# PEER block on one core: Exp, one-hot tiles, first gather rows, last two V tiles and the closing norm reordered

## The chip, the cores and the metric

The kernel runs on one NeuronCore of one Trainium2 chip. The metric is the device time of one execution in microseconds; lower is better. Only one core works, so there is no exchange between cores.

## The reference, cut to what matters

The layer is a token mixer (windowed attention beside a pooling branch, gated and merged) and then a PEER layer on 512 tokens of width 1024, with a final RMSNorm. In PEER every token picks, per head, 16 of 128 x 128 experts, and each expert is one row of `u_experts` and one row of `v_experts`:

```python
sv, si = lax.top_k(sc, PEER_TOPK)                      # per half of the key
fv, fi = lax.top_k(cand, PEER_TOPK)                    # of 256 sums
idx = jnp.take_along_axis(cidx, fi, axis=-1)
g = jax.nn.softmax(fv, axis=-1)
a = jax.nn.gelu(jnp.einsum('chkd,cd->chk', u_tab[idx], xc), approximate=False)
return jnp.einsum('chk,chkd->cd', g * a, v_tab[idx])
```

Everything is float32. The kernel has each float32 product as three matmuls of a high and a low part.

## The kernel before, in words

**The four token blocks.** The 512 tokens are four blocks of 128. Block 0 (`GB`) is computed by *gathering*: for each of its 128 (head, k) slots one indirect DMA on GpSimd brings 128 rows of `u_experts` (tile `row`, four buffers), VectorE forms the dot products (L715), and later 128 rows of `v_experts` are brought and added (L719). Blocks 1 to 3 are computed *densely*, against all 16384 experts: for each of 128 tiles of experts, `u_part` multiplies a U tile with the three blocks (24 matmuls, L105 to L107 with output `mm`) and ScalarE takes the Gelu (L604); `mix` multiplies by a gate tile (L640) and splits the product into high (L642, ScalarE) and low (L110, VectorE); `v_mm` multiplies it with the V tile into the accumulators `acc` (18 matmuls). Each U or V tile is loaded on SyncE's queue (L117), its high part is cast on ScalarE (L118), its low part taken on VectorE (L110). A token's gates are zero except at its 128 chosen experts.

**The stages.** Mixing and projections end near 360 us; `scores` near 475. In the *route* stage (to about 970 us) `part()` computes U tiles ahead of need, 4.3 us of TensorE each, and keeps their Gelu in SBUF or in HBM (`ahead`). Between the parts the program spends a budget of work on VectorE and ScalarE, by a cost that each step states: first `select` for block 0 (top-16, indices, softmax weights), then `select` and `onehot` for blocks 1 to 3 (the Background `bg`), and beside those the gathering (`fetch`, 1.1 units for each part, a dot or an add counts 1). `onehot` makes, in 16 builds per block, one-hot tiles `ohj` and `ohi` of eight tokens each; a matmul of the two (L584, output `pg`) is the gate tile, copied by ScalarE (L585) and stored to HBM. Every second `ohj` is made by ScalarE (eight Abs, L568, and a Relu, L569), the others by VectorE (L571). `ohi` is VectorE's (L574).

**The dense stage** begins with `open_dense` (the V tile and gate tiles of tile 0), six more parts (`TAIL`), the function `mix` that ends tile 0, and then `dense`, the loop over the V tiles. After it `final` makes the RMSNorm of each block: for each half an add of the accumulator (L742) and a Square with a sum (L743), the sum (L744), Sqrt (L745, another table of ScalarE than Gelu's or Exp's), a reciprocal (L746), and for each half the scaling (L748) and a store (L749).

**What sets the order.** Each engine runs its instructions in one fixed order. A planner makes it before the run: it keeps a reckoning of its own of when inputs are ready, gives each engine the instruction that is ready in that reckoning, and among several the one written earlier. `tc.high_priority(HP)` lets the U tiles of a part count as written earlier. `tc.issue_after(x)` puts what is written in its block behind the instruction x in the queue, for those instructions alone that run on the engine of x. `tc.manual_schedule` keeps the listed engines in the written order.

In `select`, `g` is the difference to the largest score (L517, VectorE); Exp (L525, ScalarE) is written ahead of the third of six pieces of the index search (L528 to L531, VectorE), and the sum of the weights (L535) behind the last.

Of the kernel before, what the change touches and what calls it, by code (L numbers as in the profile page):

```python
# [19 lines left out]
P = 128  # L20
# [29 lines left out]
G_B = 3.0  # L50
AHEAD = 60
HP = 400
U_S = 4
# [8 lines left out]
class Layer:  # L62
# [427 lines left out]
    def select(self, tp, sv, si, ei, g):  # L490
# [30 lines left out]
        for k0, k1, nh, pos, cand in ((0, 8, 4, self.fewpos, few), (8, 16, 2, self.iota[:, :NCAND], ce)):  # L521
            nk, w = k1 - k0, cand.shape[2]
            for h in range(0, PH, nh):
                if k0 == 8 and h == 0:
                    nc.scalar.activation(g, g, AF.Exp)  # L525
                hs, shape = slice(h, h + nh), [P, nh, nk, w]
                eq = tp.tile(shape, F32, name="eq", tag="k4", bufs=4)
                v.tensor_tensor(eq, pos.unsqueeze(1).unsqueeze(1).to_broadcast(shape),  # L528
                                ff[:, hs, k0:k1].unsqueeze(3).to_broadcast(shape), op=ALU.is_equal)
                v.tensor_tensor(eq, eq, cand[:, hs, :].unsqueeze(2).to_broadcast(shape), op=ALU.mult)  # L530
                v.reduce_sum(ef[:, hs, k0:k1], eq, axis=AX.X)  # L531
                yield (2.2 if k0 == 0 else 2.8) * SC
# [17 lines left out]
    def onehot(self, tp, c, jf, g):  # L550
# [12 lines left out]
        def build(n):  # L563
            u = 8 * n
            ohj = tp.tile([P, 8, P], F32, name="ohj", tag="k4", bufs=4)
            if n % OHN < OHA:
                for z in range(8):
# [30 lines left out]
    def u_part(self, n, w, xn2, keep=False):  # L598
# [3 lines left out]
        else:  # L602
            ga = self.ga.tile([P, TD], F32, name="ga", tag="ga", bufs=4)
        self.nc.scalar.activation(ga, ps, AF.Gelu)  # L604
        if keep and n >= RES:
# [10 lines left out]
    def gate_tile(self, n, q, parts=4):  # L616
        b = n // NI
        if q == 0:
# [3 lines left out]
                               in_=self.spill[s, :, n:n + NI, :].rearrange("g p i t -> p g (i t)"))  # L622

    def v_mm(self, n, w, v, acc):
        for c in range(ND):
            sl = slice(c * P, (c + 1) * P)
            for i in range(2):
                cl = slice(i * 512, (i + 1) * 512)
                self.mm3(acc[c][:, i, :], (w[0][:, sl], w[1][:, sl]), (v[0][:, cl], v[1][:, cl]),
                         n == 0, n == NKEY - 1)  # L630

# [34 lines left out]
    def dense(self, ahead, xn2, acc, fetch):  # L666
# [6 lines left out]
        def rate(m):  # L673
            return G_V if m < ahead else G_B

        last = NKEY - 2
        scale = (2 * PH * TOPK - fetch.spent) / sum(rate(m) for m in range(1, last))
        for m in (0, 1):
            u_load(m)
        for n in range(NKEY):  # L680
            m = n + 1
            if m == NKEY:
                pass
            elif m < ahead:
                step = self.mix(m, ahead)
# [7 lines left out]
            else:  # L693
# [4 lines left out]
                for _ in self.mix(m, ahead):  # L698
                    pass
            self.v_mm(n, self.ws.pop(n), self.vs.pop(n), acc)  # L700

    def gather(self, b, xn2, ei, g):
# [10 lines left out]
        def dot(s):  # L713
            u = rows(a["u_experts"], s)
            nc.vector.scalar_tensor_tensor(u, u, 1.0, xn2, op0=ALU.mult, op1=ALU.mult, accum_out=act[:, s:s + 1])  # L715

        def add(s):
            v = rows(a["v_experts"], s)
            nc.vector.scalar_tensor_tensor(z, v, act[:, s:s + 1], z, op0=ALU.mult, op1=ALU.add)  # L719

        for h in range(PH + 1):
            for k in range(TOPK):
# [11 lines left out]
    def final(self, b, y, g, acc=None):  # L734
        nc = self.nc
        t = self.rows.tile([P, D], F32, name="fin", tag="row")
        ss = self.s.tile([P, 2], F32, name="ssf")
        sd, r = (self.s.tile([P, 1], F32, name=n) for n in ("sdf", "rf"))
        halves = [slice(i * 512, (i + 1) * 512) for i in range(2)]
        for i, c in enumerate(halves):  # L740
            if acc is not None:
                nc.vector.tensor_tensor(y[:, c], acc[:, i, :], y[:, c], op=ALU.add)  # L742
            nc.scalar.activation(t[:, c], y[:, c], AF.Square, accum_out=ss[:, i:i + 1])  # L743
        nc.vector.tensor_tensor(ss[:, :1], ss[:, :1], ss[:, 1:], op=ALU.add)  # L744
        nc.scalar.activation(sd, ss[:, :1], AF.Sqrt, bias=self.eps, scale=1.0 / D)  # L745
        nc.vector.reciprocal(r, sd)  # L746
        for c in halves:
            nc.vector.scalar_tensor_tensor(t[:, c], y[:, c], r, g[:, c], op0=ALU.mult, op1=ALU.mult)  # L748
            nc.sync.dma_start(out=self.a["out"][0, b * P:(b + 1) * P, c], in_=t[:, c])  # L749

    def run(self):
# [60 lines left out]
        with tc.tile_pool(name="dense", bufs=2, reuse_waits="tile") as self.dp:  # L812
# [4 lines left out]
            nc.sync.dma_start(out=gf, in_=a["ln_final_g"].partition_broadcast(P))  # L817
            for _ in range(TAIL):
                with tc.issue_after(part()):
                    fetch.spend(G_A)  # L820
            mix()
            with tc.manual_schedule(engines={mybir.EngineType.PE, mybir.EngineType.DVE, mybir.EngineType.Activation}):
                self.dense(ahead, xn2, acc, fetch)
            fetch.spend(1e9)
            self.final(GB, self.hg, gf)
            for c in range(ND):
                hb = dp.tile([P, D], F32, name="hb", tag="vr", bufs=RAW)
                nc.sync.dma_start(out=hb, in_=self.hspill[c])
                self.final(DB + c, hb, gf, acc[c])

# [65 lines left out]
```

## Time and profile before

| | before |
|---|---|
| three runs | 1636.01, 1636.36 and 1644.2 us, median 1636.36 |
| profiled execution: span from the first to the last instruction | 1638.0 us |
| profiled execution: own time | not given beside the span; of the three runs only the one of 1644.2 us is longer than the span |
| TensorE (PE) busy | 1593.2 us |
| VectorE (DVE) busy | 1260.9 us |
| ScalarE (ACT) busy | 760.3 us |
| GpSimd (POOL) busy | 323.0 us |
| mean granted clock of TensorE | 0.992 |

All times are microseconds from the start of the span unless marked ns. A line of the timeline is start, duration, engine, line, operation, output and inputs, and in brackets the time for which the engine had stood idle before and what released it. An engine that waits in one instruction holds everything behind it in its queue. TensorE is busy for 97% of the span, so a change is worth what it takes from TensorE's idle time, or what it adds.

### The profile page before, as it was taken

To read this page: it belongs to the slowest core of one execution; us is meant where nothing else is said; L and a number is where in the kernel's file an instruction comes from. 1 tells how busy PE (TensorE), PEld (TensorE's weight loads), DVE (VectorE), ACT (ScalarE), POOL (GpSimd) and SP (SyncE) were. 2 spreads that over 40 slices of the span, in tenths; PEclk is the share of its full clock that TensorE was granted. 3 is DMA by queue.
4 is the path that set the end of the run, shared out by engine and by line. 5 is a ranking of instruction groups with operands and counts; after the bars stand their busy time and mean duration, and the time that the engine had idled before them with its cause. 6 is when DMAs were issued, how large, how long until landed. Compare 5 with 4: busy or idle time off the path is not lost.

```text
span 1638.0 us, 23397 instructions
## 1 busy us (share of the span) xinstructions
PE 1593.2 (97%) x8389; PEld 1411.9 (86%) x8389; DVE 1260.9 (77%) x2614; ACT 760.3 (46%) x1197; POOL 323.0 (20%) x262
## 2 busy tenths in 40 slices
PE   7999999999999899999999999999999999999997
PEld 6777788888899899999999998878888888899996
DVE  4676433546799899999999866877878878888885
ACT  4655533333333333894598863333333333433334
POOL 0000000000000334223322221221222222244440
PEclk9999999999999999999999999999999999999999
DMA  6111222531324888888988889999999999999983
GB/s 218 65 65 52 78 92 101 180 116 65 116 91 140 296 305 295 300 310 307 312 313 308 289 299 345 300 340 352 349 337 346 359 336 342 338 327 335 323 293 115
DMA packets 168117, 403.43 MB, mean 246 GB/s; under 512 B 14784, under 2 KB 87232, under 8 KB 164800
## 3 DMA queue, kind: packets, MB, share of 16 engines
q1 hardware_dynamic: 130384, 265.07, 46.1%
q0 software_dynamic: 36864, 134.23, 23.9%
q10 hardware_dynamic: 752, 2.62, 0.5%
q8 instruction: 66, 1.08, 0.3%
q14 instruction: 51, 0.42, 0.1%
HBM read 354.81 MB, written 46.53 MB: 245 GB/s over the span
## 4 chain that ended last, share of the span: by engine, by line
PE 86%; DMA 4%; DVE 4%; ACT 4%; issue 2%; SPq 0%; POOL 0%; DVEq 0%; ACTq 0%; POOLq 0%
PE mm L105 16%; PE mm L106 15%; PE mm L107 15%; PE acc L106 10%; PE acc L107 10%; PE acc L105 9%; PE pg L584 5%; DMA vr<-v_experts 2%; PE ho L105 1%; PE ho L107 1%; PE ho L106 1%; PE pss L453 1%; PE mm L368 1%; DVE wl L110 1%; ACT ohj L568 1%
## 5 line engine op out<-in xcount | busy, mean ns | idle before, releaser
L105 PE MATMUL mm<-xh,wh 128*128 128x384 f32 (+2 forms) x1424 | 503.3, 354 | 11.5 <-ACT ga L604 9.3
L107 PE MATMUL mm<-xh,wl 128*128 128x384 f32 (+2 forms) x1424 | 495.1, 348 | 1.9 <-DVE wl L110 1.9
L106 PE MATMUL mm<-xl,wh 128*128 128x384 f32 (+2 forms) x1424 | 494.8, 348 | 0.6 <-DVE xl L110 0.6
L110 DVE TENSOR_TENSOR wl<-wr,wh 128x1024 fp32r<-128x1024 f32 x187 | 228.0, 1220 | 135.7 <-ACT wh L118 123.0
L118 ACT CAST wh<-wr 128x1024 fp32r<-128x1024 f32 x187 | 195.6, 1047 | 284.9 <-PE mm L106 249.4
L709 POOL DMA_INDIRECT row<-u_experts,ei x128 | 150.0, 1172 | 885.5 <-ACT wh L118 528.2
L106 PE MATMUL acc<-vl,wh 128*128 128x512 f32 x768 | 299.9, 391 | 2.4 <-DVE vl L110 2.2
L107 PE MATMUL acc<-vh,wl 128*128 128x512 f32 x768 | 299.4, 390 | 0.0
L105 PE MATMUL acc<-vh,wh 128*128 128x512 f32 x768 | 298.8, 389 | 0.0
L105 PEld LDWEIGHTS mm<-xh,wh 128*128 128x128 f32 x1424 | 270.1, 190 | 31.0 <-ACT ga L604 10.7
L107 PEld LDWEIGHTS mm<-xh,wl 128*128 128x128 f32 x1424 | 269.8, 189 | 16.4 <-DVE wl L110 2.7
L106 PEld LDWEIGHTS mm<-xl,wh 128*128 128x128 f32 x1424 | 270.4, 190 | 13.8 <-DVE xl L110 1.1
L709 POOL DMA_INDIRECT row<-v_experts,ei x128 | 172.3, 1346 | 388.3 <-DVE hg L719 354.8
L642 ACT CAST wh<-wf 128x384 fp32r<-128x384 f32 x128 | 65.8, 514 | 322.5 <-PE acc L106 236.1
L110 DVE TENSOR_TENSOR vl<-vr,vh 128x1024 fp32r<-128x1024 f32 x128 | 156.7, 1224 | 52.8 <-ACT vh L118 49.7
L106 PEld LDWEIGHTS acc<-vl,wh 128*128 128x128 f32 x768 | 144.2, 188 | 33.9 <-DVE vl L110 4.6
L107 PEld LDWEIGHTS acc<-vh,wl 128*128 128x128 f32 x768 | 144.2, 188 | 29.8
L105 PEld LDWEIGHTS acc<-vh,wh 128*128 128x128 f32 x768 | 144.2, 188 | 29.5
L719 DVE SCALAR_TENSOR_TENSOR hg<-row,act,hg 128x1024 f32<-128x1024 f32 x128 | 163.6, 1278 | 2.9 <-DMA row<-v_experts,ei 2.5
L715 DVE SCALAR_TENSOR_TENSOR row<-row,natg 128x1024 f32<-128x1024 f32 x128 | 155.5, 1216 | 8.8 <-DMA row<-u_experts,ei 8.8
L118 ACT CAST vh<-vr 128x1024 fp32r<-128x1024 f32 x128 | 134.1, 1048 | 24.4 <-DMA vr<-v_experts 17.8
L110 DVE TENSOR_TENSOR wl<-wf,wh 128x384 fp32r<-128x384 f32 x128 | 74.0, 578 | 42.1 <-ACT wh L642 40.8
(179 smaller groups left out, 1611.6 us busy)
## 6 DMA issues: line engine op xcount, KB each, us to landing
wr<-u_blocks SPq DMA_DIRECT2D x128, 512.0 KB
vr<-v_experts SPq DMA_DIRECT2D x128, 512.0 KB
spill<-gs SPq DMA_DIRECT2D x24, 1024.0 KB
gt<-spill SPq DMA_DIRECT2D x64, 384.0 KB
ahead<-ga SPq DMA_DIRECT2D x90, 192.0 KB
gar<-ahead SPq DMA_DIRECT2D x90, 192.0 KB
wr<-w_in SPq DMA_DIRECT2D x30, 512.0 KB
wr<-w_query SPq DMA_DIRECT2D x16, 512.0 KB
```

The lines of the kernel that those rows point to most:

```text
L105: mm(out, lhsT=l[0], rhs=r[0], start=first, stop=False)
L106: mm(out, lhsT=l[0], rhs=r[1], start=False, stop=False)
L107: mm(out, lhsT=l[1], rhs=r[0], start=False, stop=last)
L110: self.lowered = self.nc.vector.tensor_tensor(lo, src, hi.bitcast(F32), op=ALU.subtract).ins
L118: self.nc.scalar.copy(hi, raw)
L368: nc.tensor.matmul(po[half * 64:half * 64 + 64], lhsT=vn[:, b - 1 + k, kv * 64:kv * 64 + 64], rhs=pT[:, k, 2 * half:2 * half + 2, :], star ...
L453: nc.tensor.matmul(pss[n][b // 2][:, b % 2, i - n, :], lhsT=qT[:, b * P:(b + 1) * P], rhs=subk[:, i, :], start=True, stop=True)
L584: nc.tensor.matmul(pg[:, z, :], lhsT=ohj[:, z, :], rhs=ohi[:, z, :], start=True, stop=True)
L642: nc.scalar.copy(wh, wf)
L709: nc.gpsimd.indirect_dma_start(out=t, out_offset=None, in_=tab, in_offset=bass.IndirectOffsetOnAxis(ap=ei[:, s:s + 1], axis=0))
L715: nc.vector.scalar_tensor_tensor(u, u, 1.0, xn2, op0=ALU.mult, op1=ALU.mult, accum_out=act[:, s:s + 1])
L719: nc.vector.scalar_tensor_tensor(z, v, act[:, s:s + 1], z, op0=ALU.mult, op1=ALU.add)
```

## The change

It has six edits. (1) In `select`, Exp is written two pieces later, inside `issue_after(seen)`, where `seen` is the `reduce_sum` (VectorE) of the piece before. (2) In `onehot` of the last block every fourth `ohj` is ScalarE's, not every second. (3) `gather` asks for its first four U rows ahead of everything and states a cost of 2.2 for it, so that the budget of two parts passes before the first dot; the total that `dense` spreads grows by the same 2.2. (4) The function `mix` is written inside `issue_after` of the Gelu of the fifth of the six `TAIL` parts. (5) The products of V tiles 126 and 127 are interleaved by accumulator: blocks 0 and 1 of the accumulators for both tiles, then the two halves of block 2; ahead of them stands a Sqrt of a constant. (6) `final` is cut into steps, and those of the three dense blocks are laid out in the order `CLOSE` on VectorE and ScalarE; the second half of each block is stored from ScalarE's queue.

```diff
+CLOSE = (0, 0, 0, 1, 1, 1, 2, 0, 2, 0, 1, 2, 0, 1, 2, 2, 1, 2, 0, 1, 2)
+FIRST = 2.2
...
-                if k0 == 8 and h == 0:
-                    nc.scalar.activation(g, g, AF.Exp)
+                if k0 == 8 and h == 4:
+                    with self.tc.issue_after(seen):
+                        nc.scalar.activation(g, g, AF.Exp)
...
-                v.reduce_sum(ef[:, hs, k0:k1], eq, axis=AX.X)
+                seen = v.reduce_sum(ef[:, hs, k0:k1], eq, axis=AX.X).ins
...
-            if n % OHN < OHA:
+            if n % (OHN if c + 1 < ND else 2 * OHN) < OHA:
...
-        self.nc.scalar.activation(ga, ps, AF.Gelu)
+        self.gelu = self.nc.scalar.activation(ga, ps, AF.Gelu).ins
...
-        scale = (2 * PH * TOPK - fetch.spent) / sum(rate(m) for m in range(1, last))
+        scale = (2 * PH * TOPK + FIRST - fetch.spent) / sum(rate(m) for m in range(1, last))
...
-            self.v_mm(n, self.ws.pop(n), self.vs.pop(n), acc)
+            if n < NKEY - 2:
+                self.v_mm(n, self.ws.pop(n), self.vs.pop(n), acc)
+        nc = self.nc
+        nc.scalar.activation(self.s.tile([P, 1], F32, name="sd"), self.eps, AF.Sqrt)
+        pair = [(n, self.ws[n], self.vs[n]) for n in (NKEY - 2, NKEY - 1)]
+        for part in ([(0, 0), (0, 1), (1, 0), (1, 1)], [(2, 0)], [(2, 1)]):
+            for n, w, v in pair:
+                for c, i in part:
+                    self.v_half(n, w, v, acc, c, i)
...
-            u = rows(a["u_experts"], s)
+            u = lead.pop(0) if lead else rows(a["u_experts"], s)
...
+        lead = [rows(a["u_experts"], s) for s in range(ROWS)]
+        yield FIRST
...
             if acc is not None:
+                yield
                 nc.vector.tensor_tensor(y[:, c], acc[:, i, :], y[:, c], op=ALU.add)
             nc.scalar.activation(t[:, c], y[:, c], AF.Square, accum_out=ss[:, i:i + 1])
+        yield
         nc.vector.tensor_tensor(ss[:, :1], ss[:, :1], ss[:, 1:], op=ALU.add)
+        nc.scalar.activation(r, ss[:, :1], AF.Sqrt, bias=self.eps, scale=1.0 / D)
+        yield
+        nc.vector.reciprocal(r, r)
+        for i, c in enumerate(halves):
             nc.vector.scalar_tensor_tensor(t[:, c], y[:, c], r, g[:, c], op0=ALU.mult, op1=ALU.mult)
+            (nc.sync, nc.scalar)[i].dma_start(out=self.a["out"][0, b * P:(b + 1) * P, c], in_=t[:, c])
+            yield
...
-            for _ in range(TAIL):
+            for t in range(TAIL):
                 with tc.issue_after(part()):
                     fetch.spend(G_A)
-            mix()
+                if t == TAIL - 2:
+                    seen = self.gelu
+            with tc.issue_after(seen):
+                mix()
...
+            with tc.manual_schedule(engines={mybir.EngineType.DVE, mybir.EngineType.Activation}):
+                last = [self.final(DB + c, hb, gf, acc[c]) for c, hb in enumerate(hbs)]
+                for c in CLOSE:
+                    next(last[c], None)
```

## Rows read from the trace of the kernel before

**Rows 1.** The head of the page: the span, and the busy time of each engine.

```profile
span 1638.0 us, 23397 instructions
PE 1593.2 (97%) x8389; PEld 1411.9 (86%) x8389; DVE 1260.9 (77%) x2614; ACT 760.3 (46%) x1197; POOL 323.0 (20%) x262
```

**Rows 2.** What TensorE waited for over the whole span: waiting and releasing line, us in total, times, longest.

```profile
PE mm L105 <- ACT ga L604: 9.3, 5, 4.5
...
PE pg L584 <- ACT ohj L569: 4.5, 5, 1.0
PE acc L106 <- DVE vl L110: 2.2, 3, 1.5
...
PE mm L107 <- DVE wl L110: 1.9, 2, 1.7
```

**Rows 3.** Busy time of each engine in stretches of 40 us: stretch, length, busy us (instructions) of PE, PEld, DVE, ACT, POOL, then granted clock, DMA share and GB/s.

```profile
560.00:600.00 40.00, 39.67 (x217) 39.68 (x218) 40.00 (x71) 13.32 (x20) 14.54 (x10) 0.94 0.89 307
...
880.00:920.00 40.00, 38.55 (x262) 37.91 (x260) 36.31 (x85) 34.14 (x56) 12.12 (x8) 1.00 0.85 308
920.00:960.00 40.00, 38.37 (x265) 38.05 (x266) 33.31 (x80) 34.36 (x56) 7.11 (x6) 1.00 0.76 275
...
1000.00:1040.00 40.00, 40.00 (x178) 33.07 (x178) 32.98 (x44) 13.74 (x20) 8.43 (x9) 1.00 0.98 345
```

**Rows 4.** The timeline from 529 to 543 us, four lines of POOL, ACT and DVE: the first row is asked for, a U tile is cast, the first dot, the low part of that U tile.

```profile
529.55 3.50 POOL L709 DMA_INDIRECT row<-u_experts,ei  x1 [528.24 <-ACT wh L118]
...
532.35 1.05 ACT L118 CAST wh<-wr 128x1024 fp32r<-128x1024 f32 x1 [2.72 <-PE mm L106]
...
538.25 1.23 DVE L715 SCALAR_TENSOR_TENSOR row<-row,natg 128x1024 f32<-128x1024 f32 x1 [6.17 <-DMA row<-u_experts,ei]
...
541.55 1.22 DVE L110 TENSOR_TENSOR wl<-wr,wh 128x1024 fp32r<-128x1024 f32 x1
```

**Rows 5.** The timeline of ACT and DVE around the Exp of block 0 (506 us) and of block 1 (546 to 566 us). The last line is the second piece of the index search in block 1.

```profile
506.74 0.31 ACT L525 ACTIVATE gw<-gw 128x128 f32<-128x128 f32 x1 [4.80 <-DVE gw L517]
...
546.80 1.05 ACT L118 CAST wh<-wr 128x1024 fp32r<-128x1024 f32 x1 [4.70 <-PE mm L106]
...
555.63 1.22 DVE L110 TENSOR_TENSOR wl<-wr,wh 128x1024 fp32r<-128x1024 f32 x1
...
557.23 0.31 ACT L525 ACTIVATE gw<-gw 128x128 f32<-128x128 f32 x1 [7.68 <-DVE gw L517]
...
565.25 0.82 DVE L530 TENSOR_TENSOR eq<-eq,few 128x640 f32<-128x640 f32 x1
```

**Rows 6.** TensorE's three longest stops between 500 and 1000 us (its timeline, the first matmul after each), and the busy time in the stretch of the U tile that follows each, columns as in rows 3. The stretch from 566.72 is a U tile with no stop ahead of it.

```profile
509.84 0.45 PE L105 MATMUL mm<-xh,wh 128*128 128x384 f32 x1 [2.19 <-ACT gk L604]
560.33 0.69 PE L105 MATMUL mm<-xh,wh 128*128 128x384 f32 x1 [4.46 <-ACT ga L604]
993.98 0.44 PE L105 MATMUL mm<-xh,wh 128*128 128x384 f32 x1 [2.64 <-ACT ga L604]
...
509.84:515.84 6.00, 6.00 (x25) 6.00 (x26) 6.00 (x8) 1.36 (x3) 0.00 (x0) 0.72 0.25 87
560.33:566.88 6.55, 6.55 (x25) 6.55 (x26) 6.55 (x9) 1.36 (x3) 2.61 (x2) 0.65 0.90 295
566.72:571.04 4.32, 4.32 (x26) 4.32 (x26) 4.32 (x6) 1.58 (x3) 0.00 (x0) 1.00 0.99 354
993.98:999.99 6.01, 6.01 (x25) 6.01 (x26) 1.62 (x3) 1.74 (x3) 1.01 (x1) 0.72 1.03 320
```

**Rows 7.** The last one-hot block. First the timeline of ACT in the third build, between its eight Abs and its Relu (a copy of a gate tile) and the Relu; then, of the tile `ohj` from 880 to 980 us, VectorE's builds (ns least, median, most) and what TensorE waited for it.

```profile
896.81 1.93 ACT L585 COPY gs<-pg 128x1024 f32<-128x1024 f32 x1
898.54 1.06 ACT L569 ACTIVATE ohj<-ohj 128x1024 f32<-128x1024 f32 x1
...
L571 DVE TENSOR_TENSOR ohj<-iota,tr x8: 1210/1218/1225, 886.4 to 959.8; 128x1024 f32<-128x1024 f32 x8
...
  PE pg L584: 4.1, 4
```

**Rows 8.** The opening of the dense stage: ACT's cast in `mix` of tile 0, the load of V tile 1 in SyncE's queue, and the cast of that tile.

```profile
993.03 0.51 ACT L642 CAST wh<-wf 128x384 fp32r<-128x384 f32 x1 [7.12 <-DVE wf L640]
...
994.33 0.42 SPq L117 DMA_DIRECT2D vr<-v_experts  x1
...
999.00 1.05 ACT L118 CAST vh<-vr 128x1024 fp32r<-128x1024 f32 x1 [4.27 <-DMA vr<-v_experts]
```

**Rows 9.** The end: the first matmul of V tile 126 (directly behind U tile 127), the low part of tile 127 in `mix`, the last matmul into the first accumulator (the 24th of the 36 of both tiles), then VectorE from the first add of an accumulator to the last scaling, and ScalarE's table load.

```profile
1619.31 0.39 PE L105 MATMUL acc<-vh,wh 128*128 128x512 f32 x1
...
1621.17 0.56 DVE L110 TENSOR_TENSOR wl<-wf,wh 128x384 fp32r<-128x384 f32 x1 [0.58 <-ACT wh L642]
...
1624.57 0.39 PE L107 MATMUL acc<-vh,wl 128*128 128x512 f32 x1
...
1624.99 2.65 DVE L742 TENSOR_TENSOR hb<-acc,hb 128x512 f32<-128x512 f32 x4 [3.26 <-PE acc L107]
...
1628.48 1.28 ACT L745 ACT_TABLE_LOAD   x1
...
1630.10 0.16 DVE L746 RECIPROCAL rf<-sdf 128x1 f32<-128x1 f32 x1 [1.03 <-ACT sdf L745]
...
1633.35 1.42 DVE L748 SCALAR_TENSOR_TENSOR fin<-hb,rf,gfin 128x512 f32<-128x512 f32 x2
```

More of the change, by code (lines that the diff above doesn't have):

```diff
@@ L622, in gate_tile, with v_half @@
                                in_=self.spill[s, :, n:n + NI, :].rearrange("g p i t -> p g (i t)"))
+    def v_half(self, n, w, v, acc, c, i):
+        sl, cl = slice(c * P, (c + 1) * P), slice(i * 512, (i + 1) * 512)
+        self.mm3(acc[c][:, i, :], (w[0][:, sl], w[1][:, sl]), (v[0][:, cl], v[1][:, cl]), n == 0, n == NKEY - 1)
     def v_mm(self, n, w, v, acc):
         for c in range(ND):
-            sl = slice(c * P, (c + 1) * P)
             for i in range(2):
-                cl = slice(i * 512, (i + 1) * 512)
-                self.mm3(acc[c][:, i, :], (w[0][:, sl], w[1][:, sl]), (v[0][:, cl], v[1][:, cl]),
-                         n == 0, n == NKEY - 1)
+                self.v_half(n, w, v, acc, c, i)
     def mix(self, m, ahead):
@@ L676, in dense @@
         last = NKEY - 2
-        scale = (2 * PH * TOPK - fetch.spent) / sum(rate(m) for m in range(1, last))
+        scale = (2 * PH * TOPK + FIRST - fetch.spent) / sum(rate(m) for m in range(1, last))
         for m in (0, 1):
             u_load(m)
-        for n in range(NKEY):
+        for n in range(NKEY - 1):
             m = n + 1
-            if m == NKEY:
-                pass
-            elif m < ahead:
+            if m < ahead:
                 step = self.mix(m, ahead)
@@ L699, in dense @@
                     pass
-            self.v_mm(n, self.ws.pop(n), self.vs.pop(n), acc)
+            if n < NKEY - 2:
[6 more added lines that the diff above has]
+                for c, i in part:
+                    self.v_half(n, w, v, acc, c, i)
     def gather(self, b, xn2, ei, g):
@@ L737, in final @@
         ss = self.s.tile([P, 2], F32, name="ssf")
-        sd, r = (self.s.tile([P, 1], F32, name=n) for n in ("sdf", "rf"))
+        r = self.s.tile([P, 1], F32, name="rf")
         halves = [slice(i * 512, (i + 1) * 512) for i in range(2)]
@@ L741, in final @@
             if acc is not None:
+                yield
                 nc.vector.tensor_tensor(y[:, c], acc[:, i, :], y[:, c], op=ALU.add)
             nc.scalar.activation(t[:, c], y[:, c], AF.Square, accum_out=ss[:, i:i + 1])
+        yield
         nc.vector.tensor_tensor(ss[:, :1], ss[:, :1], ss[:, 1:], op=ALU.add)
-        nc.scalar.activation(sd, ss[:, :1], AF.Sqrt, bias=self.eps, scale=1.0 / D)
-        nc.vector.reciprocal(r, sd)
-        for c in halves:
+        nc.scalar.activation(r, ss[:, :1], AF.Sqrt, bias=self.eps, scale=1.0 / D)
+        yield
+        nc.vector.reciprocal(r, r)
+        for i, c in enumerate(halves):
             nc.vector.scalar_tensor_tensor(t[:, c], y[:, c], r, g[:, c], op0=ALU.mult, op1=ALU.mult)
-            nc.sync.dma_start(out=self.a["out"][0, b * P:(b + 1) * P, c], in_=t[:, c])
+            (nc.sync, nc.scalar)[i].dma_start(out=self.a["out"][0, b * P:(b + 1) * P, c], in_=t[:, c])
+            yield
     def run(self):
@@ L824, in run @@
             fetch.spend(1e9)
-            self.final(GB, self.hg, gf)
-            for c in range(ND):
-                hb = dp.tile([P, D], F32, name="hb", tag="vr", bufs=RAW)
+            for _ in self.final(GB, self.hg, gf):
+                pass
+            hbs = [dp.tile([P, D], F32, name="hb", tag="vr", bufs=RAW) for _ in range(ND)]
+            for c, hb in enumerate(hbs):
                 nc.sync.dma_start(out=hb, in_=self.hspill[c])
-                self.final(DB + c, hb, gf, acc[c])
+            with tc.manual_schedule(engines={mybir.EngineType.DVE, mybir.EngineType.Activation}):
+                last = [self.final(DB + c, hb, gf, acc[c]) for c, hb in enumerate(hbs)]
+                for c in CLOSE:
+                    next(last[c], None)
 class Background:
```

## The prediction

> **What bounds the kernel now.** The head of the page comes first: TensorE is busy for 1593.2 of 1638.0 us [rows 1], so a change can win only what TensorE stands still, what it runs slowly, and the two ends. The waits of TensorE come second: in the middle it waited mostly for ScalarE's Gelu (9.3 us in five stops, and the stop of 2.19 [rows 6]), for a one-hot tile of ScalarE's (4.5), for low parts of U tiles (1.9) and of V tiles (2.2) [rows 2]. None of these is a shortage of ScalarE, which is busy for 46% of the span: the engine stood in front of one instruction whose input was late, with the Gelu behind it. The timeline says which. In block 1 Exp stood for 7.68 us for VectorE's difference `gw` [rows 5], and TensorE then 4.46 us for a Gelu; in block 0 Exp stood 4.80 us and TensorE 2.19; where the dense stage opens, the cast in `mix` stood 7.12 us [rows 8] and TensorE 2.64 [rows 6]. Third, the stretches behind these stops: the U tile that follows takes 6.00, 6.55 and 6.01 us in place of 4.32, at a mean granted clock of 0.72, 0.65 and 0.72 [rows 6], so part of it at 1.2 GHz after TensorE had stood still. Each of these stops costs itself and 1.7, 2.2 and 1.7 us more.
>
> **First rows asked for early.** The first dot stood 6.17 us for its row, asked for at 529.55, and behind it in VectorE's queue the low part of a U tile that had been cast at 532.35 was taken only at 541.55 [rows 4], 9.2 us after the cast. TensorE's whole 1.9 us for `wl` [rows 2] is of this place. The lag stayed: the low part at 555.63 belongs to the cast at 546.80, 8.8 us after it, and `gw` stands directly behind that, which is why Exp waited there [rows 5]. After the change the request is where it was and the first dots are two parts later, 2 x 4.32 = 8.6 us against 538.25 - 529.55 = 8.7 us from request to landing. So nearly all of the wait goes, and Exp's wait for `gw` falls by as much, from 7.68 to about 1.5 us (that two dots fewer, 1.2 us each, stand ahead of `gw` I leave as reserve). Two pairs of wait and stop, 4.80 to 2.19 and 7.68 to 4.46 [rows 5, 6], say that some 2.6 to 3.2 us of such a wait cost TensorE nothing, so 1.5 us stops nothing. Gain: 1.9 + 4.46 + 2.2 = 8.6 us. If block 1 comes to wait as block 0 does (4.80), the stop is 2.19 and 1.7 of slow clock remain, and the gain is 8.6 - 3.9 = 4.7. Four buffers of `row` are filled early, as they were. About two row pairs move to the dense stage; each costs VectorE some 1.2 us of time that it has there (33 of 40 us busy) and the DMA engines, 0.98 busy [rows 3], 0.5 MB at 345 GB/s, an estimate of 1.5 us. All V tiles together made TensorE wait 2.2 us in 128 tiles [rows 2]: I take 0, at most 3 us lost.
>
> **Exp written later.** Does this move Exp? `issue_after(seen)` binds only instructions on the engine of `seen`, which is VectorE; Exp is ScalarE's, so it gets no edge. What remains is a later place in the writing, and the planner takes what is ready by its reckoning: in block 1 Exp ran at 557.23, 8 us ahead of a step of the second piece (565.25), behind which it was written [rows 5]. It was early against its place already, so a place two pieces later should leave it where it is. I take 0. If it does move, block 0 saves its 2.19 + 1.7 = 3.9 us. Below nothing: Exp late holds VectorE at the sum of the weights (the second rival).
>
> **One-hot tiles in the last block.** ScalarE puts the copy of a gate tile (1.93) between a build's Abs and its Relu, which ends at 899.60, and the matmul waits for it: 4.1 us in four times [rows 7]. This is the third of sixteen builds, and the four are four builds apart (builds 2, 6, 10 and 14, counted from 0); after the change ScalarE keeps 0, 4, 8 and 12, so these four go to VectorE. All 4.1 us go, if VectorE has the time: it takes four builds of 1.22 = 4.9 us [rows 7], and stands idle for 80 - 36.3 - 33.3 = 10.4 us of the 80 here [rows 3]; 10.4 - 4.1 - 4.9 leaves 1.4. That is narrow, so the bounds are 4.1 gained and 4.1 - 4.9 = 0.8 lost. I take 4.1: a cast waits for TensorE to free its buffer (as in rows 4), so U tiles are made as far ahead as the buffers allow, and a low part can be 1 or 2 us late unseen.
>
> **`mix` behind the fifth Gelu.** Here the block's edge does hold: its ScalarE instruction, the cast at 993.03, and the `seen` Gelu are on one engine. The cast stood for the product with the gate tile [rows 8] and held the Gelus behind it. Behind the Gelu it holds none that TensorE needs: the sixth part starts at 991.35 in place of 993.98 and ends at 995.7, while tile 0's high part is there at 993.5 [rows 8] and its low part, I estimate, by 995. Gain: 2.64 + 1.7 = 4.3 us. Late next is V tile 1: its load was given out at 994.33, just behind the held cast and the first Gelu after it (SyncE stores that Gelu's output ahead of the load), and its cast came at 999.00 [rows 8]; the first tile's products would end at 995.7 + 4.1 = 999.8. With the Gelu free the store and the load go out some 5 us sooner, so this is covered; without that TensorE would wait some 1.5 us for V tile 1 (the cast ends at 1000.05, the low part as much again and some later). Bounds 2.8 to 4.3.
>
> **The pair and the end.** The pair computes the same 36 matmuls at (1624.57 - 1619.31) / 23 = 0.229 us each, 8.2 us, so TensorE ends where it did; its first 12 need only tile 126 and take 2.7 us, in which tile 127's Gelu, product and split (1619.31 to 1621.73, 2.4 us [rows 9]) are done. Accumulators 0 and 1 are ready six matmuls, 1.4 us, sooner. VectorE then works without a break, bar 1.03 us for Sqrt and its table load of 1.28, from 1624.99 to 1634.77. With the table loaded ahead the 1.03 goes, but a new wait can come: the first add began at 1624.99, when the matmul of the *second* half ended (1624.57 + 0.39), though it reads only the first [rows 9]. If an add waits for both halves, the first add of the third block stands until TensorE's end and holds the scalings behind it. Counted through in the order of `CLOSE` (an add 2.65 / 4 = 0.66, a scaling 1.42 / 2 = 0.71, ScalarE's Square as long as an add) VectorE ends 0.2 us sooner with that wait, 1.2 sooner without. I take 0.5; a reload for the early Sqrt or a store from ScalarE's queue (0.34 us for one issue) in front of the last Sqrt could make it 1 us worse. The Trainium skill ("ScalarE: Activation LUTs", "What ACT_TABLE_LOAD costs") puts a change of table at 1.28 us of load and about 1.38 of drain, 2.66 together. The trace has only the load before Sqrt: 1628.48 + 1.28 = 1629.76, and Sqrt's result releases VectorE at 1630.10. By that rule the end would win up to 1.0 us more, by the row nothing; the row decides.
>
> **Sum.** 8.6 + 0 + 4.1 + 4.3 + 0.5 = 17.5 us against the profiled execution. Its span is 1638.0, and of the three runs only that of 1644.2 is longer, so if it is one of the three there are 6.2 us around the span; it would come to 1626.7. The median run is 7.8 us shorter, and no trace tells whether it had the slow stretches, of which the sum holds 2.2 + 1.7 = 3.9 us. With them it comes to 1636.4 - 17.5 = 1618.9, without to 1636.4 - 13.6 = 1622.8. I forecast the middle, 1620.8, with its own range 1616 to 1626. Chance 0.53.
>
> **Rivals.** *Exp does move, and well:* the forecast and 2.2 to 3.9 us more, near 1617.5. For it: a later place in the writing is a lower rank among ready instructions. Against it: the missing edge, and that Exp ran far ahead of its place. Chance 0.14.
>
> *Exp moves and holds VectorE* (the one on the other side). Exp then comes late to the sum of weights, VectorE stands, and the low parts of the U tiles with it. One such hold of 6.17 us, the first row's, cost 8.6 us all told. If each of four blocks held VectorE as long, 4 x 8.6 = 34.4 us are lost against 17.5 + 3.9 won: 1636.4 + 13.0 = 1649. It decides from 21.4 / 4 = 5.4 us per block on. Against it: two pieces remain behind Exp, six steps of some 0.8 us [rows 5], an estimate of 4.9 us of cover. Chance 0.05.
>
> *VectorE is the bound of the route stage.* It is busy 40.00 of 40 us from 560 to 600 [rows 3]. Then the freed time is only backlog: Exp in block 1 waits as before, and the extra one-hot tiles eat their gain. What is left is 1.9 + 4.3 + 0.5 = 6.7 us: 1629.7. Against it: TensorE was busy for 39.67 us in that stretch. Chance 0.17.
>
> *The planner's new order makes stops of its own.* Each edit shifts what is written earlier, and an order fits the old waits by chance. Stops like those of rows 6 (3.9 to 6.7 us each with their slow clock) would take back most: three of them leave 1632 to 1636. Chance 0.11.
>
> **Chances.** A measurement of this kernel can tell about 0.5% (8.2 us) from no change, so faster means below 1628.2. The forecast, the first rival and the better fifth of the last two give 0.73; the rest of those two, 0.21, is the same; slower is 0.06. The range of 1613 to 1633 reaches from the first rival with all of the clock (1618.9 - 3.9 = 1615) and a better end (up to 2 us) to the middle of the last one; the costs bounded above (3 us for rows, 4.9 for one-hot tiles) lie inside it.
>
> **What would show it.** Right: no DMA wait of some 6 us at the first dot and a low part within 4 us of its cast; no stop of 4.46 us for the Gelu near 556; the stop of 2.19 at 507 still there with Exp waiting 4.8 us (if it is gone, Exp moved); no four stops of 1 us for `ohj` between 890 and 965; no stop of 2.64 us at the opening, and V tile 1 cast before it is needed; no table load behind TensorE's last matmul. Wrong: new stops for `wl` in the route stage, VectorE standing at L535, or V tiles later in the dense stage.

## The result and the profile after

The changed kernel takes 1623.85 us (median of six runs, 1620.54 to 1627.92), the kernel before took 1636.78 beside it: ratio 0.9915 [0.9898, 0.9933], so it is 0.85% faster, by 12.9 us between the medians and 13.9 by the ratio.

The head of the page, after the change. It answers to [rows 1]:

```profile
span 1621.8 us, 23361 instructions
PE 1587.7 (98%) x8389; PEld 1408.5 (87%) x8389; DVE 1265.5 (78%) x2618; ACT 749.2 (46%) x1162; POOL 316.6 (20%) x262
```

TensorE's waits over the whole span, after (waiting and releasing line, us in total, times, longest). They answer to [rows 2]:

```profile
PE mm L107 <- ACT ga L607: 8.0, 5, 2.2
PE mm L107 <- ACT gk L607: 2.2, 1, 2.2
...
PE acc L108 <- DVE vl L112: 0.2, 1, 0.2
```

The 4.5 us for one-hot tiles and the 1.9 for low parts of U tiles are gone, the 2.2 for V tiles are 0.2; the Gelu's 9.3 have only become 8.0. With block 0's stop of 2.19 these sum to 20.1 us before and 10.4 after: 9.7 us won. Which Gelus are still late is seen in TensorE's timeline, at the first matmul after each stop of over 1.5 us:

```profile
509.40 0.44 PE L107 MATMUL mm<-xh,wh 128*128 128x384 f32 x1 [2.19 <-ACT gk L607]
553.27 0.45 PE L107 MATMUL mm<-xh,wh 128*128 128x384 f32 x1 [2.00 <-ACT ga L607]
609.78 0.45 PE L107 MATMUL mm<-xh,wh 128*128 128x384 f32 x1 [2.16 <-ACT ga L607]
977.48 0.45 PE L107 MATMUL mm<-xh,wh 128*128 128x384 f32 x1 [1.83 <-ACT ga L607]
```

The first three are the Exp of blocks 0, 1 and 2; the timeline's rows of these three Exp (ScalarE), of the first request (GpSimd) and of the first dot (VectorE) answer to [rows 4, 5]:

```profile
506.29 0.31 ACT L528 ACTIVATE gw<-gw 128x128 f32<-128x128 f32 x1 [4.81 <-DVE gw L519]
...
529.11 3.18 POOL L719 DMA_INDIRECT row<-u_experts,ei  x1 [527.79 <-DVE sf L503]
...
538.16 1.22 DVE L725 SCALAR_TENSOR_TENSOR row<-row,natg 128x1024 f32<-128x1024 f32 x1 [2.31 <-DMA row<-u_experts,ei]
...
550.16 0.31 ACT L528 ACTIVATE gw<-gw 128x128 f32<-128x128 f32 x1 [4.61 <-DVE gw L519]
...
606.68 0.31 ACT L528 ACTIVATE gw<-gw 128x128 f32<-128x128 f32 x1 [4.73 <-DVE gw L519]
```

The first dot waits 2.31 us in place of 6.17, and Exp of block 1 waits 4.61 in place of 7.68. The Exp of block 0 stands as it did. Block 2's stop is new: before the change it waited 2.77 us and TensorE stood for 0.17. In each case the stop is the wait less 2.6 us (4.81 to 2.19, 4.61 to 2.00, 4.73 to 2.16): so much of it TensorE doesn't feel.

The same stretches behind the stops as in [rows 6] (columns as there):

```profile
509.70:515.70 6.00, 6.00 (x36) 6.00 (x35) 6.00 (x8) 2.42 (x4) 0.00 (x0) 1.00 0.32 97
553.20:559.20 6.00, 5.93 (x34) 5.93 (x35) 6.00 (x9) 2.78 (x5) 2.69 (x2) 1.00 0.94 311
609.77:615.77 6.00, 5.99 (x25) 5.99 (x26) 6.00 (x7) 1.35 (x3) 3.49 (x2) 0.72 0.81 249
977.48:983.48 6.00, 6.00 (x34) 6.00 (x35) 3.90 (x6) 1.64 (x4) 0.94 (x1) 1.00 1.10 300
```

In this execution only one of the four stops is followed by a stretch partly at 1.2 GHz, and it is not the longest: after 2.19 us of standing the granted clock stayed at 1.00, after 2.16 us it fell to a mean of 0.72. This matters for what a saved stop is worth (e1 below).

The opening of the dense stage on ScalarE, against [rows 8]:

```profile
975.05 1.05 ACT L120 CAST vh<-vr 128x1024 fp32r<-128x1024 f32 x1 [6.42 <-DMA vr<-v_experts]
...
976.95 0.86 ACT L607 ACTIVATE ga<-mm 128x384 f32<-128x384 f32 x2
982.00 0.50 ACT L607 ACTIVATE ga<-mm 128x384 f32<-128x384 f32 x1 [4.19 <-issue]
982.39 0.92 ACT L646 CAST wh<-wf 128x384 fp32r<-128x384 f32 x2
```

The cast in `mix` (L646) did move behind the Gelu at 982.00. But now the cast of V tile 0 stands 6.42 us for its load, two Gelus behind it, and TensorE stops for 1.83.

The end, against [rows 9], on ScalarE (first line) and VectorE (the add of the third block's first half, the last reciprocal):

```profile
1605.52 1.28 ACT L705 ACT_TABLE_LOAD   x1
...
1612.07 0.69 DVE L755 TENSOR_TENSOR hb<-acc,hb 128x512 f32<-128x512 f32 x1 [1.36 <-PE acc L109]
...
1616.24 0.16 DVE L761 RECIPROCAL rf<-rf 128x1 f32<-128x1 f32 x1 [0.36 <-ACT rf L759]
```

The table load lies ahead of TensorE's last matmul (1612.04), and Sqrt holds VectorE 0.36 us in place of 1.03. The add of the third block's first half waits 1.36 us and starts at 1612.07, when TensorE has ended, though its own half was done six matmuls (1.4 us) earlier.

### The profile page after: what moved, and what is told of

Read it like the earlier page. It is cut to its first block, busy times and chain, and to the rows that moved or that the text cites. A ratio compares the mean times of both kernels' runs of the same rounds, so it can differ in the third digit from the quotient of the medians.

```text
span 1621.8 us, 23361 instructions
## 1 busy us (share of the span) xinstructions
PE 1587.7 (98%) x8389; PEld 1408.5 (87%) x8389; DVE 1265.5 (78%) x2618; ACT 749.2 (46%) x1162; POOL 316.6 (20%) x262
## 4 chain that ended last, share of the span: by engine, by line
PE 84%; DVE 9%; ACT 2%; DMA 1%; issue 1%; SPq 1%; POOL 0%; DVEq 0%; ACTq 0%
PE mm L107 14%; PE mm L108 14%; PE mm L109 14%; PE acc L108 11%; PE acc L109 10%; PE acc L107 10%; PE pg L587 5%; DVE wl L112 2%; PE ho L107 1%; PE ho L109 1%; PE ho L108 1%; DVE row L725 1%; ACT t L352 1%; PE pss L455 1%; PE mm L370 1%
## 5 line engine op out<-in xcount | busy, mean ns | idle before, releaser
L108 PEld LDWEIGHTS mm<-xl,wh 128*128 128x128 f32 x1424 | 268.6, 189 | 13.3 <-DVE xl L112 0.7
L719 POOL DMA_INDIRECT row<-v_experts,ei x128 | 166.3, 1299 | 365.1 <-DVE hg L729 337.9
L646 ACT CAST wh<-wf 128x384 fp32r<-128x384 f32 x128 | 65.7, 514 | 306.7 <-PE acc L108 234.0
L112 DVE TENSOR_TENSOR vl<-vr,vh 128x1024 fp32r<-128x1024 f32 x128 | 156.7, 1224 | 54.1 <-ACT vh L120 54.0
```

What stands on the lines that cost most here:

```text
L108: mm(out, lhsT=l[0], rhs=r[1], start=False, stop=False)
L112: self.lowered = self.nc.vector.tensor_tensor(lo, src, hi.bitcast(F32), op=ALU.subtract).ins
L646: nc.scalar.copy(wh, wf)
L719: nc.gpsimd.indirect_dma_start(out=t, out_offset=None, in_=tab, in_offset=bass.IndirectOffsetOnAxis(ap=ei[:, s:s + 1], axis=0))
```

## The experiments

Times are medians, ratios stand against the kernel before on the same chip (its medians there: 1638.3 for e1 to e8, 1639.6 for e9 and e10).

**e1: Exp written where it was.** The changed kernel without the edit of Exp.

```diff
-                if k0 == 8 and h == 4:
-                    with self.tc.issue_after(seen):
+                if k0 == 8 and h == 0:
+                    if True:
                         nc.scalar.activation(g, g, AF.Exp)
```

> The changed kernel with Exp written where it was before the change. Theory (Exp's edit moved nothing, since the named instruction is on VectorE and Exp on ScalarE): the queues are the same as those of the changed kernel, so the ratio to before is that of the changed kernel, 0.9915 +- 0.003, about 1623 us, with the same Exp waits of 4.8, 4.6, 4.7 and 2.3 us and stops of TensorE of 2.2, 2.0 and 2.2 us. Rival (the edit shortened Exp's waits): the waits grow, and the time by 2 to 6 us.

1626.57 us, ratio 0.9918 [0.9897, 0.994]. The order of instructions on all five engines is that of the changed kernel: the edit does nothing at all, since the edge names a VectorE instruction and Exp is ScalarE's. So e1 is a second measurement of one and the same program, and shows what such a program varies by: its six executions took 1623.8 to 1629.1 us, the changed kernel's 1620.5 to 1627.9. Exp of block 1 waits 3.00 us here:

```profile
549.66 0.31 ACT L528 ACTIVATE gw<-gw 128x128 f32<-128x128 f32 x1 [3.00 <-DVE gw L519]
...
508.93:514.93 6.00, 6.00 (x25) 6.00 (x26) 6.00 (x8) 1.36 (x3) 0.00 (x0) 0.72 0.27 87
```

The last line is the stretch behind block 0's stop: 2.18 us of standing and a mean clock of 0.72, where the changed kernel had 2.19 and 1.00. Its span is 1627.3 us at a mean clock of 0.993, the changed kernel's 1621.8 at 0.997. A stop of 2 us is followed by a slow stretch in some executions and not in others.

**e2: Exp really bound.** The edge names the last Gelu, which is on Exp's engine.

```diff
-                    with self.tc.issue_after(seen):
+                    with self.tc.issue_after(self.gelu):
```

> The changed kernel with Exp bound behind the Gelu of the part written just before it (ScalarE's own queue) in place of the sum on VectorE. Theory: Exp now really moves some five U tiles later, its four waits for the difference go to 0, the three stops of 2.2, 2.0 and 2.2 us and the slow clock that follows some of them go: 6.3 us of stops, and 0 to 5 us of clock, so 1613 to 1617 us, ratio about 0.987. Rival of the prediction (Exp late holds VectorE at the sum of the weights): VectorE stands at that sum by over 2 us in each block, low parts come late, new stops of TensorE appear, and the time is 1623 us or more.

1625.2 us, ratio 0.9911 [0.9883, 0.9938]. From its trace, Exp of block 0, the first request and first dot, and TensorE's longest stop:

```profile
518.75 0.31 ACT L528 ACTIVATE gw<-gw 128x128 f32<-128x128 f32 x1
...
529.73 4.64 POOL L719 DMA_INDIRECT row<-u_experts,ei  x1 [528.41 <-ACT wh L120]
...
542.01 1.23 DVE L725 SCALAR_TENSOR_TENSOR row<-row,natg 128x1024 f32<-128x1024 f32 x1 [5.56 <-DMA row<-u_experts,ei]
...
544.44 0.47 PE L109 MATMUL mm<-xh,wl 128*128 128x384 f32 x1 [2.99 <-DVE wl L112]
```

No Exp waits for anything now and the stops at 507 and 607 are gone; VectorE does not stand at the sum of the weights either, so Exp late is no danger here. But in this execution the first row took 12.3 us from request to dot, the dot waited 5.56, TensorE stood 2.99 for the low part behind it, and 1.62 at 588 for a Gelu behind block 1's later Exp. The expected 1613 to 1617 us did not come; the six executions lie at 1620 to 1622 (three) and 1628 to 1631 (three), and the trace is of one of the longer. Alone this edit shows no gain.

**e3, e4, e5: one edit alone on the kernel before.** e3 has the early rows with their `yield FIRST`, e4 the one-hot edit, e5 the edge of `mix` behind the fifth Gelu:

```diff
+        lead = [rows(a["u_experts"], s) for s in range(ROWS)]
+        yield FIRST
```

> The kernel before with the first four rows asked for early alone. Theory: the wait of the first dot falls from 6.2 to about 2.5 us and the low part behind it no longer waits, so the stops of 1.7 and 0.2 us go and the stop of 4.5 us for the Gelu behind Exp falls to about 2: 4.4 us of stops and 0 to 2 us of slow clock, 1630 to 1633 us. As forecast the stop would go as well: 1628. Rival (VectorE is the bound of the route stage): 0 to 2 us, 1635 or more.

1630.33 us, ratio 0.9947 [0.9928, 0.9965], 8.7 us. Exp of block 1 waits 1.57 us, as forecast, and TensorE does not stand for it beyond 0.23. The first wait for a row and the Exp of blocks 1 and 2, from its timeline:

```profile
538.29 1.23 DVE L716 SCALAR_TENSOR_TENSOR row<-row,natg 128x1024 f32<-128x1024 f32 x1 [1.05 <-DMA row<-u_experts,ei]
...
547.52 0.31 ACT L526 ACTIVATE gw<-gw 128x128 f32<-128x128 f32 x1 [1.57 <-DVE gw L518]
...
604.03 0.31 ACT L526 ACTIVATE gw<-gw 128x128 f32<-128x128 f32 x1 [4.70 <-DVE gw L518]
```

The long wait of block 2 belongs to this edit: it is here without any of the others. TensorE stands 2.12 us for it.

```diff
-            if n % OHN < OHA:
+            if n % (OHN if c + 1 < ND else 2 * OHN) < OHA:
```

> The kernel before with fewer one-hot tiles from ScalarE in the last block alone. Theory: the four stops of 1.0 us go and nothing else changes, 4.1 us, 1632 to 1633 us, with VectorE 4.9 us busier between 880 and 965 us. Rival (VectorE has no time for them): stops for low parts of U tiles take their place, 1636 us or more.

1635.02 us, ratio 0.9977 [0.9961, 0.9993], 3.8 us. The four stops for `ohj` between 890 and 965 us are gone, and TensorE has no other stop of over 0.3 us there.

```diff
-            mix()
+            with tc.issue_after(seen):
+                mix()
```

> The kernel before with the function mix behind the fifth Gelu of the tail alone. Theory: two ScalarE instructions stood ahead of the Gelus at the opening of the dense stage, the cast of the gate product (L642) and the cast of V tile 0 that waits for its load; the edit moves the first and leaves the second, so TensorE's stop of 2.6 us falls to 0 to 2 us (with the load's arrival) and the gain is 0.6 to 2.6 us plus up to 1.7 of clock: 1633 to 1637 us. As forecast (only the product's cast stood there) the stop goes, 4.3 us.

1638.62 us, ratio 0.9996 [0.9982, 1.0009]: nothing. ScalarE's casts of V tiles 0 and 1, and the stop that is left:

```profile
982.85 1.05 ACT L118 CAST vh<-vr 128x1024 fp32r<-128x1024 f32 x1 [4.20 <-DMA vr<-v_experts]
...
997.04 1.05 ACT L118 CAST vh<-vr 128x1024 fp32r<-128x1024 f32 x1 [4.79 <-DMA vr<-v_experts]
...
999.40 0.50 PE L106 MATMUL acc<-vl,wh 128*128 128x512 f32 x1 [0.77 <-DVE vl L110]
```

The stop of 2.64 is gone in this profile and 0.77 us for V tile 1's low part is new. Yet the time is that of before, within 1.5 us lost and 2.9 won, outside the expected 1633 to 1637. The profiled execution (1634.76) is one of the three shortest of ten, 1633.6 to 1634.8; the other seven took 1637.9 to 1640.5, and what stood there no trace shows.

**e6: the cast of V tile 0 moved too, and another order of the end.**

```diff
-CLOSE = (0, 0, 0, 1, 1, 1, 2, 0, 2, 0, 1, 2, 0, 1, 2, 2, 1, 2, 0, 1, 2)
+CLOSE = (0, 0, 0, 1, 1, 0, 1, 2, 0, 1, 2, 2, 0, 1, 2, 1, 2, 2, 0, 1, 2)
...
         def finish():
-            v_low()
+            self.split(raw, hi, lo)
             for _ in step:
                 pass
```

> The changed kernel with the cast of V tile 0 also behind the fifth Gelu, and another order at the end: the scaling of the first block ahead of the third block's adds. The two places are read apart. Theory at the opening: the stop of 1.8 us for the Gelu goes. Theory at the end (an add waits for both halves of its accumulator, so VectorE stood idle 1.4 us ahead of the third block's first add): the tail from TensorE's end to the end of the span falls from 9.76 to about 8.7 us. Together 2.9 us and up to 1.7 of clock: about 1620 us, ratio 0.989 to 0.990. Rival at the opening: tile 0 of the dense stage comes late by its cast (1.0 us) and low part (1.2), and the stop moves there.

1623.58 us, ratio 0.9909 [0.9892, 0.9925]. The end gains: from TensorE's last matmul to the span's end 8.36 us against 9.76. The opening does not, and the expected 1620 us is missed. ScalarE's cast of V tile 0, VectorE and TensorE there:

```profile
977.92 1.04 ACT L102 CAST vh<-vr 128x1024 fp32r<-128x1024 f32 x1
...
980.36 1.03 DVE L644 TENSOR_TENSOR wf<-gk,gt 128x384 f32<-128x384 f32 x2 [7.92 <-DMA gt<-spill]
981.31 1.28 DVE L732 SCALAR_TENSOR_TENSOR hg<-row,act,hg 128x1024 f32<-128x1024 f32 x1
982.50 1.22 DVE L112 TENSOR_TENSOR vl<-vr,vh 128x1024 fp32r<-128x1024 f32 x1
...
983.78 0.50 PE L108 MATMUL acc<-vl,wh 128*128 128x512 f32 x1 [1.75 <-DVE vl L112]
```

No Gelu is late, and the low part of V tile 0 is: its cast was done at 979.0, but VectorE stood 7.92 us in front of the product for a gate tile, with the low part queued behind it.

**e7: FIRST 4.4.** The budget of four parts passes before the first dots, in place of two.

```diff
-FIRST = 2.2
+FIRST = 4.4
```

> The changed kernel with the cost of the early request stated as 4.4 in place of 2.2, so that four parts pass ahead of the first dot. Theory (two parts, 8.6 us, are just too few for a request that took 8.7 to 12.3 us, and what is left of the wait comes back at Exp of the next block): the first dot waits 0, Exp of block 1 waits 1 to 2 us, its stop of 0.4 to 2.0 us goes: 1 to 2 us less on the mean than the changed kernel, and a narrower spread; 1621 to 1624 us. Rival (VectorE is full there and Exp waits for its backlog): Exp of block 1 still waits over 3 us.

1621.52 us, ratio 0.9893 [0.9874, 0.9912]. The Exp of blocks 0, 1 and 2:

```profile
506.68 0.31 ACT L528 ACTIVATE gw<-gw 128x128 f32<-128x128 f32 x1 [4.80 <-DVE gw L519]
...
547.46 0.31 ACT L528 ACTIVATE gw<-gw 128x128 f32<-128x128 f32 x1
...
603.90 0.31 ACT L528 ACTIVATE gw<-gw 128x128 f32<-128x128 f32 x1
```

The first dot comes 13.3 us after its request and waits for no DMA, and the Exp of both later blocks waits for nothing; block 0's comes before any row and keeps its wait. The time is 2.3 us under the changed kernel's, with intervals that overlap, and 5.0 under that of e1, the same program as the changed kernel, beside the same median of before.

**e8: e2, e6 and e7 together.**

> The changed kernel with Exp bound behind a Gelu, the cost of the early request 4.4, V tile 0's cast behind the fifth Gelu and the other order at the end. Theory: all Exp waits 0, no stop at the first dot, none at the opening, tail 8.7 us: the stops between 500 and 1000 us fall from 10 to some 4 us (1.6 behind Exp's table change and two of 1.0), so 5 to 6 us of stops, 1.1 of tail and 0 to 4 of clock less than the changed kernel: 1615 to 1618 us, ratio 0.986 to 0.988. If Exp's later place only moves its stops about, 1621 us or more.

1617.11 us (1617.0 to 1621.58), ratio 0.9878 [0.9858, 0.9898]. The parts add up within this interval: the ratios of e2, e6 and e7 lie 0.0004, 0.0006 and 0.0022 under the changed kernel's, which gives 0.9883. No Exp makes TensorE stand any more, the end is that of e6, and of stops of over 0.3 us there are left 0.33 and 1.75 at the opening, 1.31 and 1.02 for a Gelu at 645 and 784, and 0.74 for a V tile.

**e9: the product behind the low part.** e8 with one more edge, to test what e6 showed.

```diff
             self.split(raw, hi, lo)
-            for _ in step:
-                pass
+            with self.tc.issue_after(self.lowered):
+                for _ in step:
+                    pass
```

> The kernel of e8 with one edit: at the opening the product with the gate tile and what follows it are queued behind the low part of V tile 0 on VectorE. Theory (order on VectorE): in e8 the cast of V tile 0 ended at 973.1, but its low part was taken only at 977.09, because VectorE stood 8.33 us for the load of a gate tile in front of the product, and the low part was queued behind the product (1.03) and an add of a row (1.28). Put ahead of the product it is made at about 973.1 to 974.3, before TensorE needs it at 976.6, and the product starts when it did (974.95): TensorE's stop of 1.75 us for the low part goes, with a part of the slow stretch behind it (some 1 to 2 us), and the time falls from 1617.1 to 1613.5 to 1615.5. Rival (arrival of V tile 0 is the limit, the order does not matter): the low part stays late and the stop of about 1.75 us stays; time 1617.

1616.02 us (1615.06 to 1616.73), ratio 0.9857 [0.9837, 0.9876], the fastest kernel here, but not the expected 1613.5 to 1615.5; against e8 the intervals overlap. VectorE and TensorE at the opening:

```profile
975.28 1.22 DVE L112 TENSOR_TENSOR vl<-vr,vh 128x1024 fp32r<-128x1024 f32 x1 [6.55 <-ACT vh L102]
977.27 1.03 DVE L644 TENSOR_TENSOR wf<-gk,gt 128x384 f32<-128x384 f32 x2 [0.76 <-DMA gt<-spill]
978.21 1.28 DVE L733 SCALAR_TENSOR_TENSOR hg<-row,act,hg 128x1024 f32<-128x1024 f32 x1
979.41 1.02 DVE L112 TENSOR_TENSOR wl<-wf,wh 128x384 fp32r<-128x384 f32 x2
...
978.42 0.50 PE L107 MATMUL acc<-vh,wh 128*128 128x512 f32 x1 [0.52 <-ACT wh L646]
980.01 0.50 PE L109 MATMUL acc<-vh,wl 128*128 128x512 f32 x1 [0.86 <-DVE wl L112]
984.86 0.50 PE L108 MATMUL acc<-vl,wh 128*128 128x512 f32 x1 [0.68 <-DVE vl L112]
```

Both theories were half right. The stop for `vl` was one of order and is gone, but the three stops that are now there (0.52, 0.86, 0.68) sum to 2.06 us, and e8 had 0.33 + 1.75 = 2.08. Behind the low part come, each just late, the gate tile (its product starts on landing, at 977.27), the product's low part behind an add of a row (1.28), and V tile 1. No slow stretch follows these short stops (granted clock 1.00 from 977 to 985), where in e8's trace the 6 us behind the stop of 1.75 have a mean of 0.72.

**e10: e8 without Exp's edge.**

> The kernel of e8 without the real edge of Exp (FIRST 4.4, the cast of V tile 0 behind the fifth Gelu, and the other order of the end stay). Theory (sum of parts): e7 measured 1621.5 and the new end is worth 1.4, so about 1620.1; Exp's edge is then worth some 3 us, which is block 0's stop of 2.18 us and a slow stretch behind it; block 0's Exp waits 4.8 us and TensorE stops 2.18 us at 507, the Exp of the blocks behind wait under 1.5 us. Rival (Exp's edge is worth nothing also beside early rows, as it was alone): 1617, with another stop in e8 in the place of the one at 507.

1619.21 us (1617.53 to 1620.55), ratio 0.9877 [0.9857, 0.9896]. Block 0's Exp waits 4.81 us and TensorE stops 2.19 us, as expected. e9, timed on the same chip in the same rounds, is 3.2 us faster and has both edges more; since e9 and e8 stop for the same time at the opening, I put most of this down to Exp, whose stop is 2.19 us. That is argued and not shown: e10's trace also has two stops for a V tile near 1088, 1.6 us in sum, that e9's has not. No run separates the two edges further: the intervals of e8, e9 and e10 overlap.

## Why the prediction came out as it did

The forecast was 1620.8 with its own range of 1616 to 1626; measured were 1623.85. The forecast case is in the main the one that happened, with one stop of its own making (block 2's, of the kind that the rival of the planner's new order names) beside it; its sum was 3.7 us too large:

| part | forecast, us | alone, us | by |
|---|---|---|---|
| first rows early | 8.6 | 8.7 (5.7 to 11.8) | e3 |
| Exp written later | 0 | 0 | e1, same order |
| one-hot tiles | 4.1 | 3.8 (1.1 to 6.4) | e4 |
| `mix` behind the fifth Gelu | 4.3 | 0.7 (-1.5 to 2.9) | e5 |
| the pair and the end | 0.5 | 0.6 | 10.32 to 9.76 us behind TensorE's end |
| sum | 17.5 | 13.8 | changed kernel: 13.9 |

(One less the ratio, times 1638.3 us, 1636.8 for the changed kernel; intervals in brackets. With intervals this wide, that 13.8 and 13.9 agree so closely is chance.)

**The step that failed is the one of `mix`.** It read the stop of 2.64 us as the wait of the cast in `mix` alone, and looked for what is late next only at V tile 1. The engine's queue held a second instruction with a late input in front of the same Gelus, the cast of V tile 0. It stood 3.36 us for its load in before's trace too, 6.2 us after the request, where no stop followed, and 6.42 after the change, 9.2 us after the request at 965.85:

```profile
983.53 1.05 ACT L118 CAST vh<-vr 128x1024 fp32r<-128x1024 f32 x1 [3.36 <-DMA vr<-v_experts]
```

TensorE's stop for the Gelu goes with this wait, trace by trace. Here are the cast and the first matmul after the stop in e4 (which leaves `mix` where it was and has another 1.46 us of stop for it), e2 and e1:

```profile
981.37 1.05 ACT L118 CAST vh<-vr 128x1024 fp32r<-128x1024 f32 x1 [6.18 <-DMA vr<-v_experts]
983.81 0.44 PE L105 MATMUL mm<-xh,wh 128*128 128x384 f32 x1 [1.59 <-ACT ga L604]
...
975.33 1.04 ACT L120 CAST vh<-vr 128x1024 fp32r<-128x1024 f32 x1 [6.58 <-DMA vr<-v_experts]
977.77 0.44 PE L107 MATMUL mm<-xh,wh 128*128 128x384 f32 x1 [1.99 <-ACT ga L607]
...
975.02 1.04 ACT L120 CAST vh<-vr 128x1024 fp32r<-128x1024 f32 x1 [6.97 <-DMA vr<-v_experts]
977.45 0.44 PE L107 MATMUL mm<-xh,wh 128*128 128x384 f32 x1 [2.38 <-ACT ga L607]
```

With the changed kernel's 6.42 and 1.83 these are four pairs, and in each the stop is the wait less 4.59 us; the waits of 3.36 to 4.56 (before, e3, e5, e7) made no such stop. So the step failed on a load that took 8.7 to 9.8 us in the four and 6.2 to 7.4 in the others; why, stays open. Where the gain went in e5 itself is open too: its one trace has the stop gone, and none of its longer executions was traced. Moving the one left the other, and moving both (e6) brought up the low part, and moving that (e9) the gate tile and V tile 1. Between 1.75 and 2.5 us are lost there in e6 to e10: several transfers, asked for at the stage's start, come in close together, and the order on the engines decides which of them TensorE stands for. That asking for them earlier would free the 2 us was not tried. The measured 0.7 also lies under the lower bound of 2.8, which counted only V tile 1; the interval just reaches it.

**First rows: right in size, partly by luck; too narrow in the cover.** The forecast set 8.6 us of cover against 8.7 from request to landing. The cover came out shorter: VectorE reached the first dot 6.7 us after the request in the changed kernel, e2 and e3, and 8.1 to 8.2 in e1 and e6. The row was used 9.05 us after the request in the changed kernel, 9.1 in e1 and 12.3 in e2. What was left of the wait helps to make Exp of block 1 wait: 1.57 us in e3, 3.00 in e1, 4.61 in the changed kernel, where the bound named for it (a stop of 2.19 as in block 0) came true with 2.00. Not foreseen at all was block 2's wait, from 2.77 to 4.73 and a stop of 2.16, with a slow stretch behind it. It comes with this edit alone (e3) and goes with twice the cover (e7). That e3 still won 8.7 us is luck in part: its trace has no slow stretch behind block 0's stop and shorter waits for V tiles, which this edit does not aim at.

**Block 2's wait is VectorE's backlog.** From the difference `gw` of block 1 to that of block 2 VectorE works without a break, 56.4 to 56.7 us in every trace; columns as in [rows 3], in the changed kernel:

```profile
549.85:606.37 56.52, 54.52 (x315) 54.20 (x314) 56.52 (x159) 21.68 (x30) 19.93 (x15) 1.00 0.92 306
```

The 13 U tiles between the two Exp take only 54.1 us where TensorE is not stopped (e6, e7, e10). So `gw` falls 2.4 us further behind the Gelu that Exp follows: from 2.8 us to 6.0 in e3 (where the tiles took 53.4), from 1.2 to 3.6 in e7. Of such a lag 1.28 us are the table load before Exp and 2.6 cost TensorE nothing, so e7's 3.6 stops nothing and e3's 6.0 stops TensorE for 2.1. Before the change TensorE lost so much time in block 1 (61.5 us for the 13 tiles) that VectorE caught up.

**Exp and the one-hot tiles** went by the steps given. The missing edge is shown in e1; that VectorE had the 4.9 us for four builds is shown by TensorE's waits after the change, which hold none for `ohj` and none for a low part of a U tile. **VectorE as the bound of the stage** falls as a forecast of the time with e3: most of the freed time reached TensorE. Between blocks 1 and 2 it holds, and there it cost the stop just named.

**The end.** The forecast lay between 0.2 with an add that waits for both halves of its accumulator and 1.2 without. The add does wait for both (1612.07, behind 1.36 us), and the gain is 0.56, and 0.5 to 0.6 in the other traces with this order. By e6 another order, with the first scaling work put into that wait, gives 1.40 more. The Trainium skill's figure ("ScalarE: Activation LUTs", "What ACT_TABLE_LOAD costs") of 1.38 us of drain beside a load of 1.28 is not seen here either: the load starts 0.02 us behind the cast ahead of it and ends at 1605.52 + 1.28 = 1606.80, and Sqrt on the same engine starts at 1606.81.

**What lies around the span.** The forecast took the profiled execution of before for the run of 1644.2, 6.2 us around its span. After the change the profiled run is 1623.65 at a span of 1621.8, 1.85 us around it, and every other run here has 1.7 to 1.9; with as much, before's execution had taken 1639.9 and was none of the listed ones. From that its 17.5 us would have led to 1622.4. Of the slow stretches the sum was right to count only a part: before's profile had three in these places and the changed kernel's one, e1, with the same program, had four.

## What to carry to other kernels

A stop for one instruction on an in-order engine is worth only the distance to the next late input in the same queue: list every instruction with its own load between the held one and the one that is needed, and say when each of those loads lands. An edge that orders "behind an instruction" binds on that instruction's engine only, so look whether both ends are on one engine before you price it. Where a transfer's cover equals its usual time, count on its slow case, and read the cover from the engine's own queue: here a stated cost of two parts left a wait for rows in four traces of five, one of four parts in one of four (e9, 1.7 us). Where two engines have about the same work in a stretch, a stop removed on one comes back as a wait for the other.

## What the runs showed of the hardware

The first indirect transfer on GpSimd, after some 528 us in which that engine did nothing, occupies it for 3.17 to 4.64 us in eleven of the twelve traces, for only 1.14 in e3; the three behind it take 0.93 to 1.50 each. From request to the first dot passed 9.05 us in the changed kernel and 12.3 in e2. One program, with the same queues, had spans from 1618.7 to 1627.3 us over the runs of the changed kernel and e1, and the longer ones have the lower mean granted clock (0.998 down to 0.993): after stops of 2.0 to 2.2 us the clock of the U tile that follows was 1.00 in some executions and 0.72 in others.
